# Seven block products for the recurrence's projection and the output projection

## The chip, the core and the metric

The kernel runs on one core of a Trainium2 chip. The metric is device time in microseconds for one execution of the whole kernel. The core's engines are PE (TensorE, matrix products into the eight PSUM banks), DVE (VectorE), ACT (ScalarE), POOL (GpSimd) and SP (SyncE, which issues the DMA transfers). Each engine works through its own queue in the order in which the program was written, and waits on semaphores for the others.

## The reference

One layer of an encoder block on x (1 x 1024 x 1024, float32), cut to what matters here:

```
z   = rms_norm(x) @ w_in                          # 1024 x 12288, split into the parts below
o_a = merge over 3 groups of dilated_window_attention(q, k, v)          # 1024 x 512
y_a = (o_a * silu(g_a)) @ w_proj_a                # 512 x 1024
o_b = rms_norm(o_fwd + o_bwd) * hg_norm_w * silu(g_b)                   # 1024 x 1024, gated recurrence both ways
y_b = o_b @ w_proj_b                              # 1024 x 1024
merged = sigmoid(zgate_a) * y_a + sigmoid(zgate_b) * y_b
out = x + merged @ w_out                          # 1024 x 1024
```

## The kernel before

Products of float32 accuracy are made of three products of the fast 32-bit type: an operand is split into a high part (ACT copies it into the type) and a low part (DVE or POOL subtracts the high part), and PE adds high x high, high x low and low x high into one PSUM bank. So one page of weights (128 x 512, 256 KB, loaded by SP) costs one ACT and one DVE or POOL instruction of 128x512, and each of its four 128x128 tiles is used in three matmuls of 128x512.

The program is not written by hand in its final order. A builder (`Builder`, with `Plan` as its clock) emits PE's work in sequence and, between the matmuls, those tasks of the other engines whose operands its cost model says are ready (`tick`); all times of the model only fix the order. Rings (`Ring`) are fixed numbers of buffers used in turn: `get` takes the next buffer, `done` gives it back, `soon` asks whether the next is free. All helpers record through one line, so the profile shows line 56 nearly everywhere, and instructions are told apart by tile names: `whi`, `wlo` (weights, a ring of `RING = 9` pairs), `sh`, `sl` (operands), `gp` (a PSUM bank).

The kernel has three stages. The first makes the norm and the input projection for attention, with seven block products in place of eight for many weight pages (`run_quads`). The second runs the recurrence among the remaining input projections and stores its result, per head, to a scratch in DRAM (`out_transpose`, `store(obD[h, u], t)`). The change is in the third stage, which begins where `hctx.close()` stands:

- Attention's projection: 16 units (8 column blocks j x 2 halves of the tokens) of 4 x 3 = 12 matmuls. `evac_ya` multiplies the bank by sigmoid(zgate_a) on DVE, into tile `ma`. The operand comes from scratch `oaD` (`split_load`, tiles `ld`, `sh`, `sl`), the gates from scratch `sgD` (`sig_load`, tiles `sgl`, ACT makes the sigmoid), four buffers.
- The recurrence's projection: 16 units of 8 x 3 = 24 matmuls; the operand from scratch `obD`, all 16 pages split once and kept. `evac_yb` multiplies by the gate (DVE), adds `ma` (POOL), and splits the sum for the next product (ACT `mh`, DVE `ml`). The recurrence's norm weight `hwc` is applied to the weight pages in their split (`b.scales`).
- The output projection: 16 units (8 blocks of 128 tokens x 2 halves of the columns) of 24 matmuls; `evac_out` adds x out of the bank on DVE and stores.

The order of loops is column block, then half (`for j in range(8): for half in range(2):`), so a weight page is used twice and given back. PSUM is dealt out as three banks for these units (`gps`, tile `gp`) and five for everything else (`bank`), as it was in the second stage. The weight pages of this stage are part of the kernel's one list of pages, loaded into a ring of four raw buffers in order; their low parts are made by POOL, or by DVE where there is a scale.

Of the kernel before, what the change touches and what calls it, by code (L numbers as in the profile page):

```python
# [572 lines left out]
def hybrid_block(ctx, tc, a, out):  # L573
# [69 lines left out]
    items += [wpa[i] for i in range(8)] + [wpb[i] for i in range(16)] + [wo[i] for i in range(16)]  # L643
# [5 lines left out]
    for i in range(16):  # L649
        b.scales[b.ops - 32 + i] = hwc  # L650
# [1178 lines left out]
    def out_transpose(h, u, on):  # L1829
# [5 lines left out]
        a_.activation(t, ps, AF.Copy)  # L1835
# [17 lines left out]
    OA, OB = {}, {}  # L1853
    ectx = {}

    def end_start():
        bctx.close()
        ectx["ep"] = ep = ctx.enter_context(tc.tile_pool(name="end", bufs=1))
        ectx["ld"] = b.ring(ep, "ld", 6, [128, 512])
        for k in range(8):  # L1860
            b.task("sp", [oaD], lambda k=k: split_load(OA, k % 4, k // 4, oaD[k % 4, k // 4],
                                                       lambda n: ep.tile([128, 512], F32R, tag="L", name=n, bufs=17)),
                   4, ectx["ld"].soon)

    def split_load(to, j, half, src, new):
        t = ectx["ld"].get()
        s_.dma_start(t, src)
        b.task("act", [t], lambda: split_store(to, j, half, t, new), 4)

    def split_store(to, j, half, t, new):  # L1870
        hi, lo = new(b.name("sh")), new(b.name("sl"))
        a_.activation(hi, t, AF.Copy)
        v_.tensor_tensor(lo, t, hi.bitcast(F32), op=OP.subtract)
        ectx["ld"].done(t)
        to[j, half] = (hi, lo)

    n = 0
# [11 lines left out]
    assert pos == b.ops - 40, pos  # L1889
# [4 lines left out]
    ep = ectx["ep"]  # L1894
    ob = ctx.enter_context(tc.tile_pool(name="endo", bufs=1, side="right"))
    MA, MH, ML = {}, {}, {}
    for half in range(2):
        for h in range(8):
            k = 8 * half + h
            b.task("sp", [obD], lambda h=h, half=half: split_load(  # L1900
                OB, h, half, obD[h, half], lambda n: ob.tile([128, 512], F32R, name=n)), 4, ectx["ld"].soon)
    def sig_load(w, j, half):
        t = ep.tile([128, 512], F32, tag="sg", name=b.name("sgl"), bufs=4)
        s_.dma_start(t, sgD[w, j, half])
        b.task("act", [t], lambda: (a_.activation(t, t, AF.Sigmoid), open_.add((w, j, half))), 1)
        return t

    def three(wp, xs, c):
        (wh, wl), (xh, xl) = wp, xs
        return [(wh[:, c:c + 128], xh), (wh[:, c:c + 128], xl), (wl[:, c:c + 128], xh)]  # L1910

    def evac_ya(j, half, sg):
# [29 lines left out]
    k = 0  # L1942
# [155 lines left out]
```

## Time and profile before

| | us |
|---|---|
| times of three runs | 1539.01, 1541.7, 1544.57 |
| median | 1541.7 |
| profiled execution: span from the first to the last instruction | 1541.9 |

| engine | busy us | share of the span |
|---|---|---|
| PE | 1502.3 | 97% |
| PE weight load | 1232.8 | 80% |
| DVE | 964.9 | 63% |
| ACT | 806.4 | 52% |
| POOL | 433.2 | 28% |

The span is the profiled execution's own time; nothing else of it is recorded around the instructions, and it stands 0.2 us above the median. PE's matmuls are pipelined: a row shows 0.39 us for a matmul that takes PE less from start to start. The page gives shares over the whole span; what a stage is limited by is read from windows and from the chain of waits. In a row of instructions, `out<-in` names tiles, then come shapes, the count, busy time and the mean of one, and the idle time before them with what ended it.

### The profile page before, as it was taken

What the parts mean: (1) busy time and instruction counts of PE and PEld (TensorE: products, weight loads), DVE (VectorE), ACT (ScalarE), POOL (GpSimd) and SP (SyncE); (2) the same over time, 40 slices, a digit from 0 to 9 for tenths busy, and PEclk for the clock granted to TensorE, in tenths of its full rate; (3) what the DMA queues carried; (4) which work ended last, traced back from release to release, by engine and by line L of the source; (5) the groups of instructions that cost most, each with busy time, mean ns of one, the idle gap of its engine ahead of it and who ended that gap; (6) DMA issues with size and microseconds to landing.
All of it is one profiled execution on the core that took longest, in us unless ns stands there. A gap on an engine that the chain in (4) does not pass through costs nothing. (4 is left out here: it accounts for less than half of the span.)

```text
span 1541.9 us, 22959 instructions
## 1 busy us (share of the span) xinstructions
PE 1502.3 (97%) x8109; PEld 1232.8 (80%) x8109; DVE 964.9 (63%) x1937; ACT 806.4 (52%) x1665; POOL 433.2 (28%) x424
## 2 busy tenths in 40 slices
PE   8999999999999999999989999999989999999999
PEld 7788888777778787888867788878878878888887
DVE  6791778687887834544333558889888886633211
ACT  5542667566676646776722255556554742733210
POOL 0022333232334230110113452444233432013320
PEclk9999999999999999999989999999999999999999
DMA  5443242442424457564256531131311312933232
GB/s 197 132 164 111 97 142 84 135 120 61 135 69 110 109 163 242 191 214 150 83 150 216 173 117 41 42 100 52 96 28 42 109 49 68 328 107 105 84 119 92
DMA packets 163767, 186.05 MB, mean 121 GB/s; under 512 B 42763, under 2 KB 99107, under 8 KB 163652
## 3 DMA queue, kind: packets, MB, share of 16 engines
q1 hardware_dynamic: 156228, 184.13, 38.2%
q10 hardware_dynamic: 7424, 0.45, 0.3%
q8 instruction: 64, 1.05, 0.3%
q14 instruction: 51, 0.42, 0.1%
HBM read 128.60 MB, written 60.66 MB: 123 GB/s over the span
## 5 line engine op out<-in xcount | busy, mean ns | idle before, releaser
L56 POOL TENSOR_TENSOR wlo<-raw,whi 128x512 fp32r<-128x512 f32 x119 | 160.6, 1356 | 431.6 <-ACT whi L56 412.0
L56 POOL TENSOR_TENSOR wlo<-qraw,whi 128x512 fp32r<-128x512 f32 x100 | 139.8, 1406 | 293.0 <-ACT whi L56 263.6
L56 PE MATMUL gp<-whi,hh 128*128 128x512 f32 x344 | 141.2, 411 | 2.8 <-ACT hh L56 1.4
L56 ACT ACTIVATE whi<-raw 128x512 fp32r<-128x512 f32 x136 | 85.0, 625 | 104.7 <-PE gp L56 79.4
L56 PE MATMUL gp<-hh,whi 128*128 128x512 f32 x336 | 137.8, 410 | 0.0
L56 PE MATMUL gp<-whi,hl 128*128 128x512 f32 x344 | 135.9, 395 | 1.3 <-DVE hl L56 1.3
L56 PE MATMUL gp<-wlo,hh 128*128 128x512 f32 x344 | 135.6, 394 | 0.0
L56 PE MATMUL gp<-hh,wlo 128*128 128x512 f32 x336 | 132.0, 393 | 0.0
L56 PE MATMUL gp<-hl,whi 128*128 128x512 f32 x336 | 131.6, 392 | 0.0
L56 ACT ACTIVATE whi<-qraw 128x512 fp32r<-128x512 f32 x140 | 86.0, 624 | 54.0 <-DVE qraw L56 33.6
L56 DVE CUSTOM_DVE_ANT_0 as<-sc,abias 128x192 f32<-128x192 f32 (+2 forms) x192 | 56.2, 348 | 92.8 <-PE sc L56 57.5
L56 ACT ACTIVATE stage<-gp 128x512 f32<-128x512 f32 x60 | 35.4, 594 | 113.6 <-PE gp L56 92.5
L56 ACT ACTIVATE as<-as,neg 128x192 f32<-128x192 f32 (+2 forms) x192 | 83.5, 438 | 7.9 <-DVE neg L56 7.9
L56 DVE TENSOR_TENSOR qraw<-qraw,qraw 128x512 f32<-128x512 f32 x80 | 67.3, 843 | 30.7 <-POOL wlo L56 23.6
L56 PEld LDWEIGHTS gp<-whi,hh 128*128 128x128 f32 x344 | 65.5, 190 | 24.1 <-issue 5.9
L56 PEld LDWEIGHTS gp<-whi,hl 128*128 128x128 f32 x344 | 65.4, 190 | 16.3 <-DVE hl L56 2.2
L56 PEld LDWEIGHTS gp<-wlo,hh 128*128 128x128 f32 x344 | 65.7, 191 | 12.2 <-issue 0.2
L56 PE MATMUL gp<-sh,whi 128*128 128x512 f32 x192 | 74.7, 389 | 0.0
L56 PE MATMUL gp<-sl,whi 128*128 128x512 f32 x192 | 74.7, 389 | 0.0
L56 PE MATMUL gp<-sh,wlo 128*128 128x512 f32 x192 | 74.7, 389 | 0.0
L56 PEld LDWEIGHTS gp<-hh,wlo 128*128 128x128 f32 x336 | 63.4, 189 | 14.0
L56 PEld LDWEIGHTS gp<-hh,whi 128*128 128x128 f32 x336 | 63.7, 190 | 11.4
(257 smaller groups left out, 3980.3 us busy)
## 6 DMA issues: line engine op xcount, KB each, us to landing
raw<-in_w_in_dram SPq DMA_DIRECT2D x112, 256.0 KB, 2.7
qraw<-in_w_in_dram SPq DMA_DIRECT2D x80, 256.0 KB, 4.3
qkD<-ny SPq DMA_DIRECT2D x48, 256.0 KB, 2.1
igD<-stage SPq DMA_DIRECT2D x32, 256.0 KB, 2.0
ig<-igD SPq DMA_DIRECT2D x32, 256.0 KB, 4.4
sgl<-sgD SPq DMA_DIRECT2D x32, 256.0 KB, 3.6
sgD<-stage SPq DMA_DIRECT2D x26, 256.0 KB, 2.0
ak<-qkD SPq DMA_DIRECT2D x6, 1024.0 KB, 7.9
```

Source lines behind the costliest of these rows:

```text
L56: got = f(*args, **kw)
```

## The change

Both 1024 x 1024 products of the third stage are written as 2 x 2 blocks of 512 x 512, and made from seven block products. With A the weights and X the operand, the products in their order are `SEVEN = ("11", "21", "T2", "T1", "T3", "22", "T4")`; "11", "21" and "22" use a block of the weights as it is, the T's use sums or differences of blocks, and likewise on the operand's side. Each block product is 4 x 4 tile pairs x 3 = 48 matmuls.

- Banks are held: PSUM is dealt out anew, four and four. The products 11, T2, T3, T4 add into the same four banks; 21, then T1 and 22, go into the other four. After 11, T2 and T1 ACT copies the running sum out of the bank (tiles `acc`) while it stays open; after 21, T3 and 22 DVE adds the bank to such a copy, which gives a finished quarter; T4 gives the last quarter alone.
- The sums of weights and operands (`mix`) are made by DVE in the raw tiles, one step ahead of their use, in an order of their own (`in_order`); the low parts of all pages of the stage but attention's are made by DVE (`b.low = "dve"`).
- Each operand page is split again for each product: 7 x 4 splits on the operand's side and 7 x 4 on the weights' side for each of the two products. Rings: 8 pairs `xh`/`xl` for operands, 9 pairs for weights, 18 raw weight pages (`eraw`), 8 kept sums (`acc`), 3 gate or x pages (`sg`, four before).
- In the recurrence's projection a finished quarter is multiplied by its gate (DVE, "gate") and added to `ma` by POOL ("merge"). In the output projection POOL adds x to the kept copies ("fold"), 12 instructions; for the last quarter DVE adds x out of the bank.
- Attention's loops are exchanged: half outside, column block inside.
- `hwc` is applied in the copy before the recurrence's result is stored (`out_transpose`).

The diff, cut to its core:

```diff
-    items += [wpa[i] for i in range(8)] + [wpb[i] for i in range(16)] + [wo[i] for i in range(16)]
+    items += [wpa[i] for i in range(8)]
...
-    for i in range(16):
-        b.scales[b.ops - 32 + i] = hwc
...
-        a_.activation(t, ps, AF.Copy)
+        a_.activation(t, ps, AF.Copy, scale=hwc)
...
-        ectx["ld"] = b.ring(ep, "ld", 6, [128, 512])
+        ectx["acc"] = b.ring(ep, "acc", 8, [128, 512])
+        ectx["xh"] = b.ring(ep, "xh", 8, [128, 512], F32R)
+        ectx["xl"] = b.ring(ep, "xl", 8, [128, 512], F32R)
+        ectx["sg"] = b.ring(ep, "sg", 3, [128, 512])
...
+    def split_x(t):
+        hi, lo = ectx["xh"].get(), ectx["xl"].get()
         a_.activation(hi, t, AF.Copy)
         v_.tensor_tensor(lo, t, hi.bitcast(F32), op=OP.subtract)
+        return hi, lo
...
+    psum(4)
...
+    rawq = b.ring(ob, "eraw", 18, [128, 512])
...
+    SEVEN = ("11", "21", "T2", "T1", "T3", "22", "T4")
...
+        for op in SEVEN:
+            for i in range(4):
+                m = {"T2": "11", "T1": "11", "T3": "12", "T4": "21"}.get(op, op)
+                split(op, m, i, op not in ("11", "21", "T2"))
+        for i in range(4):
+            mix("T3", i, "12", "22", "12", OP.subtract)
+            mix("T2", i, "11", "12", "11", OP.add, ("11",))
+        for i in range(4):
+            mix("T4", i, "21", "21", "11", OP.subtract, ("21",))
+            mix("T1", i, "11", "22", "11", OP.subtract, ("T2",))
+        in_order(work)
+        in_order(mixes)
...
+        for op, a, kh in (("11", 0, 0), ("21", 0, 1), ("T2", 0, 0), ("T1", 1, 0), ("T3", 0, 0), ("22", 0, 1), ("T4", 1, 1)):
+            for i in range(4):
+                split(op, kh, a, i)
+        for i in range(4):
+            mix("T3", i, (0, 0), (0, 0), (1, 0), OP.subtract, ("11",))
+            mix("T2", i, "s2", (1, 1), (0, 0), OP.subtract)
+        for i in range(4):
+            mix("T1", i, (1, 0), (1, 0), (1, 1), OP.add)
+            mix("22", i, (0, 1), (0, 1), "s2", OP.subtract, ("21",))
+        in_order(work)
+        in_order(mixes)
+        return pairs
...
+    def seven(base, pairs, tok, A, E, kept, fin, ready):
+
+        bankA, bankE, p, q, r = {}, {}, {}, {}, {}
+
+        def keep(to, op, u, ps):
+            to[u] = t = acc.get()
+            a_.activation(t, ps, AF.Copy)
+            kept(op, u, t)
+
+        def add(op, u, t, ps):
+            if ready is not None:
+                b.until(lambda: ready(op, u))
+            v_.tensor_tensor(t, ps, t, op=OP.add)
+
+        def evac(op, u):
+            if op == "11":
+                keep(p, op, u, bankA[u])
+            elif op == "21":
+                add("11", u, p[u], bankE[u])
+                E.done(bankE[u])
+                fin(0, 0, u, p[u], None)
+            elif op == "T2":
+                keep(q, op, u, bankA[u])
+            elif op == "T1":
+                keep(r, op, u, bankE[u])
+            elif op == "T3":
+                add("T1", u, r[u], bankA[u])
+                fin(1, 1, u, r[u], None)
+            elif op == "22":
+                add("T2", u, q[u], bankE[u])
+                E.done(bankE[u])
+                fin(0, 1, u, q[u], None)
+            else:
+                fin(1, 0, u, bankA[u], A)
+
+        for o, op in enumerate(SEVEN):
+            for u in range(4):
+                if op == "11":
+                    bankA[u] = A.get(name="sA")
+                elif op in ("21", "T1"):
+                    bankE[u] = E.get(name="sE")
+                out = (bankE if op in ("21", "T1", "22") else bankA)[u]
+                for k in range(4):
+                    n = base + 4 * o + (k if tok else u)
+                    b.until(lambda: b.split_next > n and (op, k) in pairs)
+                    (wh, wl), (xh, xl) = b.w[n], pairs[op, k]
+                    if tok:
+                        s = slice(128 * u, 128 * u + 128)
+                        prods = [(xh[:, s], wh), (xh[:, s], wl), (xl[:, s], wh)]
+                    else:
+                        s = slice(128 * k, 128 * k + 128)
+                        prods = [(wh[:, s], xh), (wh[:, s], xl), (wl[:, s], xh)]
+                    for i, (l, x) in enumerate(prods):
+                        t_.matmul(out, l, x, start=(op in ("11", "21", "T1") and k == 0 and i == 0),
+                                  stop=(k == 3 and i == 2), skip_group_check=op in ("T2", "T3", "22", "T4"))
+                    if tok and u == 3:
+                        b.free_to(n + 1)
+                    if u == 3:
+                        drop_x(pairs[op, k])
+                    b.tick()
+                if not tok:
+                    b.free_to(n + 1)
+                evac(op, u)
+                b.tick()
...
+    b.low = "dve"
+    seven_weights(b.ops, wB, (obs[:8], obs[8:], ()))
+    pairs_b = seven_sides(X)
...
+    seven_weights(b.ops + 28, wO)
+
+    def fin_b(half, c, u, t, bank_):
+        j = 4 * c + u
+        sg = (1, j, half)
+
+        def gate():
+            d = t if bank_ is None else sgs[sg]
+            v_.tensor_tensor(d, t, sgs[sg], op=OP.mult)
+            if bank_ is None:
+                sgr.done(sgs[sg])
+            else:
+                bank_.done(t)
+            b.task("pool", [d], lambda: merge(d), 2)
+
+        def merge(d):
+            ma = MA[j, half]
+            g_.tensor_tensor(ma, d, ma, op=OP.add)
+            (acc if bank_ is None else sgr).done(d)
+            M[half, c, u] = ma
+
+        b.task("dve", [t], gate, 1, lambda: sg in open_)
+
+    seven(b.ops, pairs_b, False, b.gps, b.bank, lambda *_: None, fin_b, None)
...
+    def fold(op, u, t):
+        def f():
+            g_.tensor_tensor(t, t, xr[op, u], op=OP.add)
+            sgr.done(xr[op, u])
+            folded.add((op, u))
+        b.task("pool", [t], f, 1, lambda: (op, u) in xr and b.when_all([xr[op, u]]))
...
+    def fin_o(half, e, u, t, bank_):
+        r0 = 128 * (4 * half + u)
+        ring, o = acc, t
+        if bank_ is not None:
+            b.until(lambda: ("T4", u) in xr)
+            ring, o = sgr, xr["T4", u]
+            v_.tensor_tensor(o, t, o, op=OP.add)
+            bank_.done(t)
+
+        def out_():
+            s_.dma_start(out[r0:r0 + 128, 512 * e:512 * e + 512], o)
+            ring.done(o)
+        b.task("sp", [o], out_, 1)
+
+    seven(b.ops + 28, pairs_o, True, b.bank, b.gps, fold, fin_o, lambda op, u: (op, u) in folded)
```

More of the change, by code (lines that the diff above doesn't have):

```diff
@@ L1888, in hybrid_block @@
     hctx.close()
-    assert pos == b.ops - 40, pos
-    ep = ectx["ep"]
+    assert pos == b.ops - 8, pos
+    psum(4)
+    ep, acc, sgr = ectx["ep"], ectx["acc"], ectx["sg"]
     ob = ctx.enter_context(tc.tile_pool(name="endo", bufs=1, side="right"))
[L1896 to L1901, printed above, removed]
+    rawq = b.ring(ob, "eraw", 18, [128, 512])
@@ L1963, in evac_out @@
[L1963 to L1993 removed]
+    AT = (("21", 0, 0), ("T3", 1, 1), ("22", 0, 1), ("T4", 1, 0))
```

202 lines of the change are left out of this document (117 added, 85 removed).

## The prediction

> **What bounds the kernel now.** I read the page first: the span, the busy shares, the 40 slices.
>
> ```profile
> span 1541.9 us, 22959 instructions
> PE 1502.3 (97%) x8109; PEld 1232.8 (80%) x8109; DVE 964.9 (63%) x1937; ACT 806.4 (52%) x1665; POOL 433.2 (28%) x424
> ...
> PE   8999999999999999999989999999989999999999
> ...
> DVE  6791778687887834544333558889888886633211
> ...
> PEclk9999999999999999999989999999999999999999
> ```
>
> PE is busy in nine tenths of every late slice at full clock; VectorE (DVE) falls to 2, 1, 1 tenths in the last three. Next the chain that ended last, its last steps:
>
> ```profile
> 1308.45 229.88 PE gp L56 x1014
> ...
> 1538.36 0.69 DVE stage L56
> ```
>
> For the last 230 us nothing but PE's own queue is on the path. The change touches the end of that stretch; the table by windows splits it into attention projection, recurrence projection (call it B) and output projection (O):
>
> ```profile
> core 0: us, PE busy (x) PEld busy (x) DVE busy (x) ACT busy (x) POOL busy (x), PEclk, DMA share, GB/s
> 1320.30:1364.00 43.70, 43.70 (x194) 36.18 (x193) 27.38 (x42) 27.16 (x45) 0.10 (x1) 1.00 0.77 255
> 1364.00:1451.00 87.00, 87.00 (x386) 72.03 (x385) 27.24 (x39) 26.88 (x46) 29.59 (x23) 1.00 0.30 94
> 1451.00:1541.90 90.90, 87.32 (x386) 71.97 (x384) 12.44 (x18) 5.58 (x9) 11.64 (x9) 1.00 0.35 107
> ```
>
> In all three PE is busy throughout. VectorE has 27, 27 and 12 us of work beside 44, 87 and 91: lots of room, and this room is what the change spends. The matmuls of the three parts, in the view of one tile (each has three kinds of equal count; the first and the last are shown):
>
> ```profile
> L56 PE MATMUL gp<-sh,whi x192: 389/389/389, 1320.6 to 1450.4; 128*128 128x512 f32 x192
> ...
> L56 PE MATMUL gp<-whi,ml x128: 388/389/389, 1451.6 to 1537.9; 128*128 128x512 f32 x128
> ```
>
> 3 x 192 + 3 x 128 = 960 matmuls start between 1320.6 and 1537.9: 217.3 / 959 = 0.2266 us each. That pace prices everything that PE loses or gains.
>
> **Part by part: what goes.** Attention's 192 matmuls stay. B and O have 384 each; seven block products of 4 x 4 tile pairs x 3 are 336 each. 96 matmuls go: 96 x 0.2266 = 21.8 us, if PE stays fed. One block product lasts 48 x 0.2266 = 10.88 us. The scale of the recurrence's norm moves into an existing copy; that costs nothing that PE could wait for.
>
> **What comes: VectorE.** Each operand page, on both sides and for each of the seven products, is split into a high part (ScalarE) and a low part (VectorE), and there are sums before the splits and after the products. Rows for the price of one:
>
> ```profile
> 1333.96 1.29 DVE L56 TENSOR_TENSOR sl<-ld,sh 128x512 fp32r<-128x512 f32 x2
> 1335.17 1.28 DVE L56 TENSOR_TENSOR ma<-gp,sgl 128x512 f32<-128x512 f32 x2
> ...
> L56 DVE TENSOR_TENSOR stage<-gp,xr 128x512 f32<-128x512 f32 x16 | 11.1, 692 | 73.2 <-PE gp L56 73.2
> ```
>
> A lone 128x512 addition is shown as 0.69 us, but two end within 1.29, and the pair at 1333.96 gives way to the next at 1335.17: 1.21 / 2 = 0.605 us per addition when they queue.
>
> In the order in which the changed program's instructions stand, VectorE's queue from the first low part of B's second product ("21") to the low part of the last weight page that O's fourth product ("T1") needs holds 177 instructions of 128x512: 81 low parts, 64 sums of operands and weights, 16 additions out of PSUM banks, 16 gate multiplications (four of these out of PSUM). The first cannot start before attention's last matmul: its buffer is one of a ring of eight pairs, still held by attention's operand. The last is wanted by PE ten products and ten matmuls after that moment: 10 x 10.88 + 2.3 = 111.1 us. VectorE needs 177 x 0.605 = 107.1 us, so even with nothing else it would be within 4 us of being the bound. ScalarE has some 12 instructions per product, and rows for it are
>
> ```profile
> 1340.15 0.63 ACT L56 ACTIVATE sh<-ld 128x512 fp32r<-128x512 f32 x1 [0.53 <-DMA ld<-obD]
> 1340.82 0.69 DVE L56 TENSOR_TENSOR sl<-ld,sh 128x512 fp32r<-128x512 f32 x1 [0.16 <-ACT sh L56]
> ...
> 1348.88 1.66 ACT L56 ACTIVATE sgl<-sgl 128x512 f32<-128x512 f32 x3
> ```
>
> Three in 1.66 us, 0.55 each: 6.6 of 10.88 us, not the bound. The first two rows show the handover: a high part at 1340.15, its low part 0.67 later. The held banks cost nothing: the two sets of four take turns, so each copy or addition out of a bank has a whole product, 10.88 us, before PE writes there again.
>
> **GpSimd's share of VectorE's time.** The program keeps 16 merges on GpSimd and adds 12 of its additions (the residual into kept partial products); 24 of the 28 lie within those 177. Rows:
>
> ```profile
> L56 POOL TENSOR_TENSOR sgl<-sgl,ma x16: 1283/1284/1289, 1370.6 to 1452.2; 128x512 f32<-128x512 f32 x16
> ...
> 1156.18 1.28 POOL L56 TENSOR_TENSOR km<-km,sk 128x512 f32<-128x512 f32 x1
> 1156.28 1.20 DVE L56 SCALAR_TENSOR_TENSOR rr<-rt,ri 128x4 f32<-128x4 f32 x1
> ...
> 1157.91 0.16 DVE L56 SCALAR_TENSOR_TENSOR rr<-rt,rr 128x4 f32<-128x4 f32 x1
> ...
> 1319.12 1.29 POOL L56 TENSOR_TENSOR wlo<-raw,whi 128x512 fp32r<-128x512 f32 x1 [6.71 <-DMA ld<-oaD]
> ...
> 1319.54 1.42 DVE L56 TENSOR_TENSOR sl<-ld,sh 128x512 fp32r<-128x512 f32 x1 [0.34 <-ACT sh L56]
> ...
> L56 DVE TENSOR_TENSOR spare<-qC,spare x12: 677/688/692, 159.7 to 496.1; 128x512 f32<-128x512 f32 x12
> ```
>
> GpSimd takes 1.28 us for one. A VectorE instruction of 128x4 that takes 0.16 us took 1.20 when it came 0.10 behind one: 1.04 us lost, until GpSimd was done. A low part that came 0.42 behind took 1.42 instead of 0.69. An addition out of a PSUM bank was never over 692 ns in the twelve of one group. So behind a queue that never empties each GpSimd addition takes about 1.04 us from VectorE: 24 x 1.04 = 25.0 us. Bounds: 0.5 each (12 us) if half of them fall on PSUM additions or on VectorE's own waits; 1.28 each (30.7 us) if all are met at their start.
>
> The Trainium skill, "SBUF — State Buffer", section "SBUF: two separate sides", says that a VectorE operation with two SBUF inputs and a GpSimd operation that reads SBUF take turns for the whole instruction, and the loser blocks fully. The rows agree in kind (1.20 instead of 0.16; nothing for PSUM sources). By its letter the sum has 30.7 for 25.0, 5.7 us more.
>
> **VectorE's own waits.** In four places of the 177 a low part stands directly behind the sum it is made of, and ScalarE must make the high part in between: about 0.75 us each; in six one instruction stands between: 0.15 each. That is 3.9. At the start the weight pages of "21" are loaded behind gate pages that wait for one of three buffers, and landing takes
>
> ```profile
> DMA to landing us min/median/max: 2.9/3.6/5.4
> ```
>
> one landing, of which I count 3 us (SP's queue is in order: the operand pages stand behind that gate page too). Together 7, bounds 2 and 12. ScalarE's first high part takes 0.7. Sum: 0.7 + 107.1 + 25.0 + 7 = 139.8 us, against 111.1: PE is 28.7 us late by O's "T1". Behind that stand 32 VectorE instructions for four products, 4.8 us in each 10.88, and PE runs freely again; lateness is not regained.
>
> A nearer point shows how this begins. The addition that empties the last bank of B's "21" can run 0.4 us after that product, at 22.2 us. From it to the low part that B's "T1" begins with are 28 instructions: 28 x 0.605 = 16.9, two GpSimd merges 2.1, two of the 0.75 waits and two of 0.15 1.8, and 0.1 until it lands: 43.1, where PE wants it at 32.6. So 10 us of the 28.7 are lost by there, about 3 inside "T2" and 7 in one gap before "T1".
>
> **The border.** The PSUM banks are dealt out anew before attention's projection, and its first matmul now waits for ScalarE's copy out of the last bank before it.
>
> ```profile
> 1320.33 0.39 PE L56 MATMUL gp<-hh,wlo 128*128 128x512 f32 x1
> ...
> 1320.56 0.39 PE L56 MATMUL gp<-sh,whi 128*128 128x512 f32 x1
> ...
> 1320.81 0.60 ACT L56 ACTIVATE stage<-gp 128x512 f32<-128x512 f32 x1 [1.30 <-issue]
> ```
>
> The copy ends at 1321.41; the matmul stood at 1320.56 and can then start at about 1321.5: 1.0 us once (bounds 0.8 and 1.3), with all of attention's matmuls queued behind it. At the far end nothing changes: a VectorE addition out of PSUM and one store behind the last matmul.
>
> **PE's clock after a gap.** Three windows around the one long gap of the trace:
>
> ```profile
> 1238.40:1241.50 3.10, 0.22 (x2) 0.02 (x1) 3.03 (x7) 0.43 (x1) 1.28 (x1) 1.00 0.10 18
> 1241.60:1244.90 3.30, 3.02 (x14) 3.02 (x15) 0.23 (x1) 0.00 (x0) 0.00 (x0) 0.50 0.15 57
> 1245.00:1248.30 3.30, 3.30 (x26) 3.04 (x25) 1.60 (x7) 0.60 (x1) 0.00 (x0) 1.00 0.00 0
> ```
>
> PE was busy 0.22 of the first 3.1 us; the next 3.3 us ran at 0.50, with 14 matmuls for 26 in the third. Half of 3.3 is lost: 1.7 us. Most of it is hidden where PE waits for VectorE again anyway; the last stall, in O's "T1", has no such cover, and may come in pieces of 1 to 4 us. I take 0.9, bounds 0 and 3.4.
>
> **The sum.** The profiled execution has a span of 1541.9 us; the median of three runs is 1541.7 (1539.01 to 1544.57), so the span stands for the median. -21.8 + 28.7 + 1.0 + 0.9 = +8.8: **1550.7 us**.
>
> **The rivals.** *PE stays nearly fed, and the kernel is faster.* If GpSimd's additions cost VectorE nothing (they fall into its waits, or on additions out of PSUM), only the sequence at B's "T1" remains: 22.2 + 16.9 + 1.8 + 0.1 = 41.0 against 32.6, 8.4 us, plus 2.0 at O's start (its first low part stands behind a weight page that needs the buffer of B's last one: 0.67 + 0.605 + 0.7), plus the border and 0.9. -21.8 + 8.4 + 2.0 + 1.0 + 0.9 = -9.5: 1532.4. For it: VectorE is 31% busy in B's window now, and the additions out of PSUM do run freely. Against it: the 1.20 and 1.42 rows, and a queue that is within 4 us of full without GpSimd. It decides at about 0.67 us for each of the 24: 24 x 0.67 = 16.1 is 8.9 less than 25.0, all of the forecast's loss. Chance 0.14.
>
> *The clock bites.* Four gaps (before B's "T1", O's start, O's "T2" and "T1") that each outlast 3 us and are followed by matmuls that PE cannot make up: 4 x 1.7 = 6.8 instead of 0.9: 1556.6. For it: the 0.50 row. Against it: while PE is behind VectorE's queue a slow matmul costs nothing. Chance 0.16.
> The Trainium skill, "TensorE: Matmul & The Clock Gate", Part 1, has the clock halved after an idle window of about 3.4 us until a busy one has passed; the 3.1 us window with its 0.22 us of work and the 0.50 row behind it agree.
>
> *The sums are not in time for lack of data.* In attention's window DMA moves 255 GB/s at a share of 0.77; the changed program also loads there the operand of B, and behind it two more sets of weight pages. If B's third product waits some 10 us longer for pages, VectorE's whole queue shifts: 1560.7. Against it: the same 255 GB/s already holds a similar number of pages. Chance 0.10.
>
> **How the numbers follow.** My forecast has 0.60. A measurement tells 0.3%, 4.6 us, from no change; "same" is 1537 to 1546. Forecast bounds: GpSimd 12 to 30.7 moves it by -13 to +5.7, waits by -5 to +5, clock by -0.9 to +2.5; not all at once, so 1540 to 1559 for it alone. The range 1540 to 1562 leaves out the faster rival (0.14) and the far end of the data rival. Faster: the first rival nearly whole and a sliver of the forecast, 0.14; same: the forecast's low end, 0.16; slower: 0.70.
>
> **What would show it.** In the changed profile: about 864 matmuls from the border to the end; VectorE over 90% busy from B's second product to O's fourth; GpSimd rows of 1.28 beside VectorE additions of 1.3 to 1.9 us; a PE gap of about 7 us before B's "T1", released by the low part of a weight page, and several of 1 to 5 us at O's start, "T2" and "T1"; clock 0.5 behind the long one; a first attention matmul about 1 us behind its predecessor. I am wrong if PE stays above 95% busy there, if VectorE additions stay at 0.69 beside GpSimd's, or if PE's waits name DMA or ScalarE's copies out of the held banks.

## The result, and the profile after

The changed kernel takes 1553.98 us (median of four runs, 1549.17 to 1556.16) against 1541.28 us for the kernel before beside it: a ratio of 1.0078, 95% interval 1.0055 to 1.0101, so 12.7 us slower. 1550.7 was forecast, in a range of 1540 to 1562. The page of the profiled execution (its own time is 1549.17 us):

```profile
span 1546.9 us, 22973 instructions
PE 1486.8 (96%) x8013; PEld 1216.6 (79%) x8013; DVE 1065.4 (69%) x2077; ACT 845.6 (55%) x1737; POOL 437.2 (28%) x420
...
DVE  6791777787877835454333459889798885378984
```

96 matmuls are gone (8013 for 8109) and PE is busy 15.5 us less, but the kernel is longer. VectorE's last three slices, once 2, 1, 1 tenths, are 9, 8 and 4. The span is only 5.0 us longer than before's, less than the medians say: attention's first matmul starts 5.7 us earlier, behind stages that the change hardly touches. PE's clock fits that: ahead of this matmul it stood at 0.50 for 20.5 us in the profiled execution of before, and for 3.4 in this one. The same place in the table by windows (columns as in the next table), of before (first row) and of after:

```profile
797.80:808.00 10.20, 9.81 (x20) 5.91 (x21) 6.77 (x8) 1.98 (x3) 2.00 (x2) 0.50 0.18 69
```
```profile
798.30:801.70 3.40, 3.40 (x8) 1.93 (x8) 1.84 (x3) 0.00 (x0) 1.27 (x1) 0.50 0.00 0
```

So I compare the changed stretch itself, from the start of attention's first matmul to the start of the last matmul ("the stage" below): 217.4 us before (1320.56 to 1537.93), 228.1 after (1314.84 to 1542.97). With the border in front of it, where the time between the starts of two matmuls grew from 0.23 to 1.23 us, that is 11.7 us, near the 12.7 of the medians. In the table by windows of after, the rows are attention's end, B's "11" and "21", B's "T2" with the gap before "T1", the rest of B, O's first four products, and O's last three:

```profile
core 0: us, PE busy (x) PEld busy (x) DVE busy (x) ACT busy (x) POOL busy (x), PEclk, DMA share, GB/s
1336.60:1358.40 21.80, 21.80 (x98) 18.07 (x97) 10.66 (x17) 10.06 (x17) 0.00 (x0) 1.00 0.60 193
1358.40:1380.20 21.80, 21.80 (x98) 18.07 (x97) 17.87 (x29) 9.60 (x17) 1.75 (x2) 1.00 0.78 273
1380.20:1403.90 23.70, 14.12 (x49) 10.33 (x48) 19.86 (x31) 11.14 (x20) 4.47 (x3) 0.83 0.13 34
1403.90:1451.80 47.90, 46.34 (x192) 37.76 (x192) 43.78 (x62) 25.53 (x46) 14.68 (x10) 0.94 0.40 126
1451.80:1510.50 58.70, 49.47 (x192) 39.23 (x193) 51.30 (x66) 25.46 (x48) 22.71 (x14) 0.88 0.24 77
1510.50:1543.20 32.70, 32.70 (x145) 26.89 (x144) 15.96 (x26) 6.74 (x13) 2.37 (x1) 1.00 0.32 113
```

Where the row's length and PE's busy time differ, PE stands: in B's "T2" and before "T1", in O's first four products, and for 1.6 us in the rest of B. PEclk below 1.00 marks the same rows. Seven products at 10.88 us, twice, behind attention's 43.6 would end the stage at 195.7; 32.4 us are lost, at six places: B's "T2" with the gap behind it 12.8 and "T1" 2.6, the passage to O 1.8, O's "11" 6.0, "T2" 0.8, "T1" 8.4. PE's new waits in the view of waits (total, times, longest):

```profile
PE sE L56 <- ACT whi L56: 9.9, 2, 6.0
...
PE sA L56 <- DVE xl L56: 4.0, 2, 3.7
PE sA L56 <- ACT whi L56: 3.6, 1, 3.6
...
PE sA L56 <- ACT xh L56: 1.6, 1, 1.6
...
PE sE L56 <- DVE wlo L56: 1.2, 1, 1.2
```

They name high and low parts, as the forecast wanted, not the copies out of the held banks. And the border, in the timeline:

```profile
1314.10 0.60 ACT L56 ACTIVATE stage<-gp 128x512 f32<-128x512 f32 x1 [0.81 <-PE gp L56]
...
1314.84 0.47 PE L56 MATMUL gp<-xh,whi 128*128 128x512 f32 x1 [0.84 <-ACT stage L56]
```

### The profile page after: what moved, and what is told of

Read it like the earlier page. It is cut to its first block, busy times and chain, and to the rows that moved or that the text cites. A ratio compares the mean times of both kernels' runs of the same rounds, so it can differ in the third digit from the quotient of the medians.

```text
span 1546.9 us, 22973 instructions
## 1 busy us (share of the span) xinstructions
PE 1486.8 (96%) x8013; PEld 1216.6 (79%) x8013; DVE 1065.4 (69%) x2077; ACT 845.6 (55%) x1737; POOL 437.2 (28%) x420
## 5 line engine op out<-in xcount | busy, mean ns | idle before, releaser
L56 POOL TENSOR_TENSOR wlo<-raw,whi 128x512 fp32r<-128x512 f32 x103 | 139.9, 1365 | 383.4 <-ACT whi L56 372.2
L56 ACT ACTIVATE whi<-raw 128x512 fp32r<-128x512 f32 x120 | 74.9, 626 | 68.9 <-PE gp L56 42.9
L56 PEld LDWEIGHTS gp<-hh,whi 128*128 128x128 f32 x336 | 63.5, 189 | 11.2
L56 PEld LDWEIGHTS gp<-hl,whi 128*128 128x128 f32 x336 | 63.4, 189 | 11.0
L56 POOL COPY mm<-Bc 128x4 f32<-128x4 f32 x96 | 41.2, 468 | 83.2 <-DVE Bc L56 81.7
L56 ACT ACTIVATE ny<-spare 128x512 f32<-128x512 f32 x50 | 31.3, 626 | 58.8 <-DVE spare L56 58.8
```

What stands on the lines that cost most here:

```text
L56: got = f(*args, **kw)
```

## The experiments

Three causes were to be told apart: GpSimd's additions that hold VectorE up (A, the prediction's); VectorE's order of work (D, its nearer point at B's "T1"); and, once the first four runs were in, late operand pages of B (E). The clock was tested last. In the recorded expectations of e1 to e4 three rivals have letters of their own: Rival B is the order and the rings without GpSimd, Rival C is ScalarE's queue behind a late gate page, and the Rival D of e3 is only that VectorE has too much work. The table has, for each run, the stage and the start of six products in us after attention's first matmul, read from the profiled execution's matmuls; the first row is PE without a gap.

| run | stage | B "T1" | B "T3" | O "11" | O "21" | O "T1" | O "T3" | time, median | ratio to before, 95% |
|---|---|---|---|---|---|---|---|---|---|
| (no gap) | 195.7 | 76.3 | 87.2 | 119.8 | 130.7 | 152.4 | 163.3 | | |
| after | 228.1 | 89.1 | 102.6 | 137.0 | 153.9 | 176.5 | 195.7 | 1553.98 | 1.0078 (1.0055 to 1.0101) |
| e1_small_pool | 212.8 | 88.5 | 102.2 | 136.0 | 147.4 | 169.2 | 180.4 | 1536.05 | 0.9976 (0.9960 to 0.9992) |
| e2_adds_on_dve | 219.1 | 87.7 | 100.1 | 134.0 | 146.9 | 169.5 | 186.7 | 1543.87 | 1.0024 (1.0008 to 1.0040) |
| e3_low_on_pool | 239.4 | 89.2 | 103.1 | 136.9 | 151.6 | 185.5 | 207.0 | 1565.91 | 1.0173 (1.0153 to 1.0193) |
| e4_four_gates | 225.9 | 89.0 | 102.3 | 136.9 | 156.2 | 178.0 | 193.5 | 1550.88 | 1.0075 (1.0048 to 1.0102) |
| e5_operand_first | 215.4 | 76.3 | 88.2 | 126.0 | 144.1 | 165.8 | 183.0 | 1541.28 | 1.0000 (0.9988 to 1.0013) |
| e6_all_three | 202.7 | 76.3 | 87.2 | 121.0 | 137.6 | 159.4 | 170.3 | 1528.86 | 0.9912 (0.9895 to 0.9928) |
| e7_order_only | 217.9 | 86.4 | 97.3 | 133.6 | 152.8 | 174.6 | 185.5 | 1543.12 | one run |
| e8_keep_warm | 230.8 | 94.5 | 105.5 | 139.4 | 157.6 | 179.4 | 198.3 | 1556.89 | 1.0094 (1.0079 to 1.0109) |
| e9_keep_warm_short | 223.2 | 88.8 | 100.0 | 134.4 | 149.9 | 175.5 | 190.8 | 1545.96 | 1.0031 (1.0017 to 1.0046) |
| e10_operand_and_order | 208.8 | 76.3 | 87.2 | 125.6 | 143.7 | 165.5 | 176.4 | 1534.25 | 0.9957 (0.9940 to 0.9973) |
| e11_operand_and_adds | 212.1 | 76.3 | 87.2 | 122.4 | 139.7 | 161.5 | 179.7 | 1535.87 | 0.9976 (0.9959 to 0.9994) |

The kernel before took 1539.8, 1541.7 and 1539.8 us in the three groups of runs (e1 to e4, e5 to e8, e9 to e11); each ratio is to its own group. The changed kernel was timed beside its own runs of before alone.

### GpSimd's additions: e1, e2, e3

e1 cuts the 28 additions to 4 of their 512 columns, leaves the rest of those sums out, and leaves each instruction in its place:

```
-            g_.tensor_tensor(ma, d, ma, op=OP.add)
+            g_.real.tensor_tensor(ma[:, 0:4], d[:, 0:4], ma[:, 0:4], op=OP.add)
...
-            g_.tensor_tensor(t, t, xr[op, u], op=OP.add)
+            g_.real.tensor_tensor(t[:, 0:4], t[:, 0:4], xr[op, u][:, 0:4], op=OP.add)
```

> GpSimd's 28 additions of the last stage (16 merges, 12 folds) are cut to 4 of their 512 columns; the rest of those sums is left out. Every instruction of every engine keeps its place. Stage = first matmul of attention's projection to the last matmul: 217.4 us before, 228.1 in the changed kernel. Theory A (GpSimd's additions hold VectorE up, about 1.04 us each for the 24 that lie in its long queue): 25 us of VectorE's time go; PE still waits some 10 us at the recurrence's T1, so the stage is 208 to 213 us and the kernel some 16 us faster than the changed one, about 1537. Rival B (the waits come from the order, the rings and ScalarE's queue; GpSimd only coincides): stage within 4 us of 228.

e2 gives the same 28 additions, whole, to VectorE:

```
-            b.task("pool", [d], lambda: merge(d), 2)
+            b.task("dve", [d], lambda: merge(d), 2)
...
-            g_.tensor_tensor(ma, d, ma, op=OP.add)
+            v_.tensor_tensor(ma, d, ma, op=OP.add)
...
-            g_.tensor_tensor(t, t, xr[op, u], op=OP.add)
+            v_.tensor_tensor(t, t, xr[op, u], op=OP.add)
...
-        b.task("pool", [t], f, 1, lambda: (op, u) in xr and b.when_all([xr[op, u]]))
+        b.task("dve", [t], f, 1, lambda: (op, u) in xr and b.when_all([xr[op, u]]))
```

> The same 28 additions, whole, are made by VectorE instead of GpSimd. Theory A: each costs VectorE 0.605 us instead of about 1.04, so the 24 in the long queue cost 14.5 instead of 25: stage about 218 us, kernel about 1544. Rival B: VectorE's queue is longer by 17 us of work and nothing is taken off it: stage 232 or more, kernel 1558 or more.

e3 goes the other way and makes the low parts of the weights on GpSimd:

```
-    b.low = "dve"
+    b.low = "pool"
```

> The low parts of the 56 weight pages of the two products are made by GpSimd instead of VectorE. Theory A: each takes 1.04 us or more from VectorE by holding it up, in place of 0.605: 37 of them lie in the long queue, +16 us: stage about 244 us, kernel about 1570. Rival D (VectorE simply has too much work, and GpSimd is free capacity): 37 x 0.605 = 22 us go from VectorE's queue: stage 206 to 212, kernel about 1534.

Stages of 212.8, 219.1 and 239.4 us: 15.3 and 9.0 less than the changed kernel, and 11.3 more, where 16 was expected. Groups of instructions on VectorE and GpSimd from 1358 us on (busy, mean ns of one), after:

```profile
L56 DVE TENSOR_TENSOR wlo<-eraw,whi 128x512 fp32r<-128x512 f32 x51 | 39.9, 802 | 15.5 <-ACT whi L56 15.2
L56 DVE TENSOR_TENSOR eraw<-eraw,eraw 128x512 f32<-128x512 f32 x32 | 27.2, 855 | 0.0
L56 DVE TENSOR_TENSOR xl<-ma,xh 128x512 fp32r<-128x512 f32 x24 | 19.6, 850 | 0.2 <-ACT xh L56 0.2
...
L56 DVE TENSOR_TENSOR acc<-sE,acc 128x512 f32<-128x512 f32 x12 | 8.1, 679 | 0.0
...
L56 POOL TENSOR_TENSOR ma<-acc,ma 128x512 f32<-128x512 f32 x12 | 18.5, 1547 | 116.5 <-DVE acc L56 116.5
```

and in e1:

```profile
L56 DVE TENSOR_TENSOR wlo<-eraw,whi 128x512 fp32r<-128x512 f32 x50 | 33.3, 687 | 15.7 <-ACT whi L56 15.4
L56 DVE TENSOR_TENSOR eraw<-eraw,eraw 128x512 f32<-128x512 f32 x32 | 21.7, 682 | 0.0
L56 DVE TENSOR_TENSOR xl<-ma,xh 128x512 fp32r<-128x512 f32 x24 | 15.6, 683 | 0.4 <-ACT xh L56 0.4
```

With whole additions on GpSimd, VectorE's three largest groups between SBUF tiles take 802 to 855 ns in the mean; with small ones 682 to 687. The group that reads a PSUM bank takes 679, and 682 in e1. GpSimd pays too: 1.55 us in the mean of this group, where one alone took 1.28. One turn in the timeline of after, in which VectorE's instruction takes 1.77 us and ends 0.5 behind GpSimd's:

```profile
1461.53 1.72 POOL L56 TENSOR_TENSOR acc<-acc,sg 128x512 f32<-128x512 f32 x1 [1.18 <-issue]
...
1462.02 1.77 DVE L56 TENSOR_TENSOR eraw<-eraw,eraw 128x512 f32<-128x512 f32 x1
```

VectorE waited only 0.8 us, once, for a result of GpSimd, so it is the turns and not late results. So A holds, and e2 says what it is worth to a program that computes everything: the stage is 9.0 us shorter with 28 more additions on VectorE (28 x 0.605 = 16.9 us). The price of the turns alone doesn't give that much: the 24 additions in the long queue would take 14.5 us on VectorE, and their turns took at most 19.6 (worked out below). VectorE also waits less for high parts in e2 (7.0 us instead of 15.2 from 1358 to 1525 us), and PE's clock stands at 0.50 for 13.7 us of the stage instead of 27.3; how much each is worth stays open. The table shows where e1 gains: nearly all of it lies in O ("11" 11.4 us long instead of 16.9, "T1" 11.2 instead of 19.2). B is nearly untouched: "T1" starts at 88.5 instead of 89.1. The loss in B, nearly half of all, is not GpSimd's.

### What holds B up: e4, e5, e7

The chain of waits of after, at that place:

```profile
1358.86 0.61 DVE ma L56
...
1359.53 0.32 SPq L56
...
1362.26 5.11 DMA ob<-obD
...
1367.47 0.70 DVE acc L56
...
1382.83 2.63 DMA sg<-sgD
...
1386.19 0.53 ACT whi L56
...
1386.77 1.22 PE sA L56 x2
```

and SyncE's queue in the timeline of after:

```profile
1357.09 0.42 SPq L56 DMA_DIRECT2D eraw<-in_w_proj_b_dram  x1
1359.53 0.32 SPq L56 DMA_DIRECT2D sg<-sgD  x1
1359.90 0.42 SPq L56 DMA_DIRECT2D eraw<-in_w_proj_b_dram  x1
1360.37 3.87 SPq L56 DMA_DIRECT2D ob<-obD  x8
```

SyncE issues in the order of its program. A gate page (sg) needs one of three buffers. The page issued at 1359.53 waited for one that VectorE frees with the last gate multiplication of attention's projection (DVE ma, 1358.86 in the chain); the second half of B's operand (ob, eight pages) stands behind it and is issued from 1360.37 on, though its last data were written to memory by an issue at 1302.5. The page on the chain is there at 1367.37, 8.9 us after B's first matmul (1358.48). VectorE is idle 1.7 us until then, and then works for 13 us nearly without a pause; 12 of its first 20 instructions are operand sums and their low parts, which it could have made earlier.

e4 gives the gate pages a fourth buffer (and takes one of eighteen from the weight pages):

```
-        ectx["sg"] = b.ring(ep, "sg", 3, [128, 512])
+        ectx["sg"] = b.ring(ep, "sg", 4, [128, 512])
...
-    rawq = b.ring(ob, "eraw", 18, [128, 512])
+    rawq = b.ring(ob, "eraw", 17, [128, 512])
```

> Four buffers for gate pages and x pages instead of three, and 17 raw weight buffers instead of 18 (there is no room for both). Theory A: VectorE sets the pace, no change: stage 225 to 231. Rival C (ScalarE stands in its queue on a sigmoid whose gate page had to wait for one of three buffers, with the weights' high parts behind it; the chain of the changed kernel shows this ahead of the 4.0 us gap in the recurrence's T2): that gap and its like go, 4 to 8 us: stage 220 to 224.

It did next to nothing: "T1" at 89.0, ratio 1.0075 for the changed kernel's 1.0078, and a stage (225.9) inside what was expected for no change. The operand pages' row in its trace (first and last issue) shows why:

```profile
L56 SPq DMA_DIRECT2D ob<-obD x16: 423/428/443, 1336.8 to 1368.3; - x16
```

The last operand page is issued 49.3 us after attention's first matmul (1318.99); in after it was 48.9 (1363.7). The queue is as before, with one more gate page ahead, and the operand still behind it. Nor did Rival C get what it needs: ScalarE still waits 3.6 us for a gate page, up to 1387.22, with the high part that opens B's "T2" (1387.76) behind it. This run speaks for neither side, since its edit did not move what it was to move.

e5 puts the operand's pages ahead of the gate pages, and of B's weight pages too, by one number in one line:

```
-                b.task("sp", [obD], f, 2, b.wire)
+                b.task("sp", [obD], f, 0.5, b.wire)
```

> The changed kernel with one edit: the pages of B's operand (its second half) go into SyncE's queue ahead of the gate pages that wait for one of three buffers, instead of behind them. Everything is computed. Where the four runs before leave it: B's loss (T2 10.9 to 12.8 us, T1 2.6) stood untouched by GpSimd's additions, so it is not theirs. Theory E (B's operand arrives too late: its last pages are issued in order behind gate pages, and VectorE has nothing to do at B's start): B's T1 begins at about 76 us after attention's first matmul instead of 89.1, O begins at 125 to 127 instead of 137.0; O's own loss remains and may even grow by 1 to 3 us, since VectorE's queue is as long as before, so the stage is 215 to 219 us instead of 228.1 and the time 1540 to 1545 us (ratio to before 1.000 to 1.003). Theory D, the prediction's own step (B's T1 is late by VectorE's order of 28 instructions and two holds by GpSimd): T1 still begins 10 us late, at 86 to 89 us, stage 225 to 228, time 1549 to 1553 us.

The pages' rows in after, and in e5:

```profile
L56 SPq DMA_DIRECT2D ob<-obD x16: 422/428/1077, 1329.9 to 1363.7; - x16
L56 DVE TENSOR_TENSOR ob<-ob,ob x8: 683/684/1189, 1365.1 to 1397.7; 128x512 f32<-128x512 f32 x8
```
```profile
L56 SPq DMA_DIRECT2D ob<-obD x16: 383/430/442, 1320.3 to 1343.2; - x16
L56 DVE TENSOR_TENSOR ob<-ob,ob x8: 681/684/690, 1347.6 to 1376.7; 128x512 f32<-128x512 f32 x8
```

Counted from attention's first matmul (1314.84 and 1320.00), the last page is issued at 23.2 instead of 48.9 us and the first sum begins at 27.6 instead of 50.3. B's "T1" starts at 76.3, without a gap, with the same number of instructions on VectorE; the stage is 12.7 us shorter. E holds. Landing takes no less than in after (3.9 us in the median, 3.7 there), so the pages were late for their place in the queue and not for the load on DMA. D, that order and holds alone would keep "T1" 10 us late, falls. And the three gate buffers are still three, so the gate page that ScalarE stands behind in after (the chain at 1382.83) looks late because VectorE, late itself, freed its buffer late.

e7 changes VectorE's order alone: operand sums for "22", and the splits of "T3" and "22", wait until the weights of "T1" are split, and the sums for "22" come behind all of those for "T1".

```
-                         and b.when_all([at()]) and ectx["xh"].soon() and ectx["xl"].soon(), f))
+                         and b.when_all([at()]) and (op not in ("T3", "22") or b.split_next >= base + 16) and ectx["xh"].soon() and ectx["xl"].soon(), f))
...
-                           and near([X[*k, i] for k in at]) and (op != "T2" or acc.soon()), f))
+                           and near([X[*k, i] for k in at]) and (op != "T2" or acc.soon()) and (op != "22" or b.split_next >= base + 16), f))
...
             mix("T1", i, (1, 0), (1, 0), (1, 1), OP.add)
+        for i in range(4):
             mix("22", i, (0, 1), (0, 1), "s2", OP.subtract, ("21",))
```

> The changed kernel with the order edit alone: operand sums for '22', and the splits of 'T3' and '22' operands, behind the splits of T1's weight pages; everything is computed. Theory E with a queue at O (order is a small part): B's T1 3 to 4 us earlier than 89.1, O's T1 product 13 us long instead of 19.2, stage 221 to 223 us instead of 228.1, time 1543 to 1548 us. Theory D (order is the cause of B's late T1): B's T1 at 79 to 81 us, stage about 218 us, time 1539 to 1543 us. If VectorE's queue is late as a whole and order is indifferent: stage 226 to 229 us, time 1549 to 1553 us.

217.9, in a single run: a larger gain than E expected (221 to 223), and D's figure for the stage, but not D's for B: "T1" comes 2.7 us earlier, not 8 to 10, and the whole wait moves into "T2" (one gap of 8.1 us). Most of what e7 gains it gains at "T1", where nothing is lost any more in either projection: 2.6 and 8.4 us in after. At O's start it loses 4.3 us more. So order is not what makes VectorE late in B; it decides whether work that nobody waits for yet stands ahead of work that PE waits for. I had undersized that.

### PE's clock: e8, e9

Dummy matmuls of 128x128 keep PE busy where it stood, written into banks that PE is about to open, so that the next matmul overwrites them (e8: 30, 52, 32 and 36 at the four places; e9: 17, 25, 15 and 18).

```
+        def keep_warm(where, n):
+            if where not in early:
+                early[where] = E.get(name="sE")
+            for _ in range(n):
+                t_.real.matmul(early[where][:, 0:128], ident, ident, start=True, stop=True)
...
+                if first and (op, u) == ("T2", 1):
+                    keep_warm(("T1", 0), 30)
+                if first and (op, u) == ("T1", 0):
+                    early[op, u] = bankE[u]
+                    keep_warm((op, u), 52)
+                    early.pop((op, u))
...
+                    if not first and (op, u, k) == ("T1", 0, 3):
+                        keep_warm((op, 1), 36)
...
+                        if not first and (op, u, k, i) == ("11", 0, 0, 2):
+                            keep_warm(("21", 0), 32)
```

> The changed kernel with dummy matmuls of 128x128 where TensorE has its gaps: 30 before T2's second unit and 52 before T1's first in B, 32 in O's 11 and 36 in O's T1, all into PSUM banks that TensorE is about to open, so that their result is overwritten; the other engines do the same work in the same order, and everything is computed. The gaps stay as late as they were, but TensorE is not idle in them. Theory 'clock' (each gap is followed by 6.8 us at clock 0.5, and at least the last, in O's T1, is not made up): no window at 0.5 at the four places, and the stage 2.7 to 6 us shorter than 228.1, 222 to 225.5 us, time 1547 to 1550 us, ratio to before 1.004 to 1.006. Theory 'the slow clock is hidden where TensorE waits for VectorE again anyway' (the prediction's 0.9 us): stage 227 to 228, time 1550 to 1553 us, ratio 1.007 to 1.009. If the dummy matmuls outlast the gaps, T1 in B begins later than 89.1 and the stage is longer than 228.1.

e8 did not decide: each dummy left two records of some 0.11 us, and 6.6 to 11.5 us of them outlasted gaps of 4.0 to 6.3 us. B's "T1" was pushed to 94.5, the stage to 230.8; what full clock gave and what the dummies took can't be parted there.

> As e8_keep_warm, with half as many dummy matmuls: there each 128x128 matmul of fp32 ran as two records of about 0.11 us, so 30, 52, 32 and 36 of them took 6.6, 11.5, 7.0 and 7.9 us, longer than the gaps that they were to fill, and delayed T1 in B to 94.5 us instead of 89.1. Now 17, 25, 15 and 18: estimated at 3.8, 5.5, 3.3 and 4.0 us, a little less than the gaps of 4.0, 6.3, 4.1 and 4.3 us. Everything is computed. Theory 'clock' (the 6.8 us at clock 0.5 behind the last gap are not made up): clock 1.0 at all four places, O's T1 product some 16 us long instead of 19.2, stage 223 to 226 us instead of 228.1, ratio to before 1.003 to 1.006. Theory 'VectorE's queue alone sets the ends' (a slow clock is hidden where TensorE waits again): O's T1 product still 18.5 to 19.2 us, stage 227 to 229 us, ratio 1.006 to 1.009.

O's last gap in after, in the table by windows (columns as above), and the same place in e9:

```profile
1494.60:1498.00 3.40, 0.50 (x1) 0.19 (x1) 3.40 (x5) 1.24 (x3) 0.97 (x1) 1.00 0.51 152
1498.00:1504.80 6.80, 5.62 (x13) 4.47 (x14) 4.14 (x7) 2.58 (x5) 2.16 (x1) 0.50 0.06 18
```
```profile
1494.00:1498.00 4.00, 4.00 (x37) 3.96 (x36) 4.00 (x6) 3.38 (x7) 1.65 (x1) 1.00 0.39 117
1498.00:1504.80 6.80, 6.74 (x31) 5.39 (x30) 3.54 (x6) 1.49 (x3) 3.95 (x2) 1.00 0.14 42
```

13 matmuls in 6.8 us at half clock against 31 (in the first, 1.2 us of the time is a wait for a low part). All four stretches at 0.50 are gone (a new one of 3.4 us came in O's "T2"), and the stage is 223.2: full clock at the four places was worth 4.9 us, net of what the dummies took, and the ratio to before is 1.0031 (1.0017 to 1.0046), clear of the changed kernel's interval. O's "T1" product took 15.3 us, where the theory of the clock had 16 and the other 18.5 to 19.2. The other theory is right about the stretches before it: e9 leads by 4.0 us at O's "21" and by 1.0 at "T1" (the table), because "T2" took 14.7 us instead of 11.7: PE, earlier, waited for VectorE there, and ran 3.4 us of it at 0.50.

### Together: e10, e11, e6

e10 has the edits of e5 and e7, e11 those of e5 and e2, e6 all three.

> The changed kernel with the operand pages of B ahead of the gate pages and with the order edit, GpSimd's 28 additions left where they are; everything is computed. Alone the two took 12.7 and 10.2 us from the stage of 228.1; all three edits left 202.7. If the two losses are separate, 22.9 us go: stage about 205 us. If order mostly moved the same lateness (what it took at B was the operand's), only its part at O is left, 4 to 7 us: stage 208 to 212 us, time 1533 to 1537 us, ratio 0.994 to 0.997. And GpSimd's additions then still cost the difference to 202.7, 5 to 9 us, about all of it at O's start, where VectorE's queue stays full.

> The changed kernel with the operand pages of B ahead of the gate pages and GpSimd's 28 additions on VectorE, without the order edit; everything is computed. Alone the two took 12.7 and 9.0 us. If they are separate, as theory E and the holds say (operand at B, holds at O): stage 206 to 210 us, B's T1 at 76.3, O's T1 product still 15 to 18 us long for want of the order edit, time 1530 to 1535 us, ratio 0.993 to 0.996. If VectorE's queue only shifts its lateness from one product to the next: stage 213 us or more, ratio 0.998 or more.

> The changed kernel with three edits, everything computed: the operand pages of B ahead of the gate pages (as in the run before this one), the 28 additions of GpSimd on VectorE (as in e2_adds_on_dve), and VectorE's sums and splits reordered so that those of '22' and the splits of 'T3' and '22' stand behind the splits of T1's weight pages. If the three losses are separate and each edit takes its own away (operand late 13 us, GpSimd's holds 9 net of the moved work, order 4 or so): stage 202 to 205 us instead of 228.1, 24 us less, the time 1526 to 1530 us, ratio to before 0.991 to 0.993. If VectorE's queue as a whole is the bound, and the edits only shift which product waits (the loss removed at B comes back at O): stage 212 to 219 us, time 1536 to 1543 us, ratio 0.998 to 1.002.

Alone the three edits take 12.7 (operand), 10.2 (order) and 9.0 us (additions) from the stage; in pairs 19.3 and 16.0 instead of 22.9 and 21.7; together 25.4 instead of 31.9. So they are mostly separate, and a part looks like one lateness that each of them can take away. e10 came out as the second of its expectations, and its 6.1 us behind e6 stand at O's "21" already (143.7 and 137.6): GpSimd's additions at O's start; e11 (212.1) lies between its two, nearer the one in which VectorE's queue shifts its lateness on. e6 is 0.9912 of before (0.9895 to 0.9928), 12.8 us faster than the kernel before and 25 faster than the changed one. Its chain through B:

```profile
1366.15 10.88 PE sA L56 x48
1377.03 10.88 PE sE L56 x48
1387.91 10.88 PE sA L56 x48
1398.79 10.88 PE sE L56 x48
```

"11", "21", "T2" and "T1" are back to back. What is left of the loss is 7 us at O's start, where VectorE is full; 2.7 of them are the clock's, since the 46 matmuls behind the last wait took 13.1 us, where 10.4 would do. The table by windows of e6:

```profile
1443.30:1492.70 49.40, 46.42 (x193) 37.90 (x194) 47.89 (x80) 24.06 (x44) 0.00 (x0) 0.93 0.26 84
```

80 instructions, 47.9 of 49.4 us: VectorE's queue, which the prediction priced, now makes PE wait there alone.

## Why the prediction was right, and where it was not

**The matmuls, the border: as forecast.** 864 matmuls start in the stage, 96 fewer; a product without a gap takes 10.88 us in every run. The border cost 1.00 us for a forecast of 1.0.

**VectorE's queue: right in its length, wrong in what it is made of.** The forecast had the low part that O's "T1" needs 139.8 us behind attention's end, where PE wants it at 111.1. In after that matmul, the fourth page's second, starts at 1499.18, 140.7 us behind B's first at 1358.48. One row holds the stretch:

```profile
1358.40:1498.90 140.50, 120.41 (x492) 96.23 (x490) 128.46 (x180) 67.08 (x121) 38.86 (x24) 0.92 0.37 119
```

180 VectorE instructions for 177 counted, 24 GpSimd additions for 24, VectorE 91% busy. But the terms: 180 x 0.605 is 108.9, so GpSimd's turns made at most 19.6 us of the 128.5 (0.82 each, not 1.04: 25.0), and VectorE stood 12.0 us, not 7. The two errors, each about 5 us, nearly cancel: that the total came out is in part luck.
The Trainium skill, "SBUF — State Buffer", section "SBUF: two separate sides", with turns of a whole instruction, gives 30.7 for that term (an estimate, 24 x 1.28). The trace agrees with it in kind (802 to 855 ns against 679 for PSUM sources, and GpSimd's own 1.55 for 1.28) and not in amount. In the timeline of that stretch 21 VectorE instructions last longer than 0.69 us, by 18.2 us in all (near the 19.6), and each ends 0.55 us behind an addition of GpSimd. Ten of the 24 additions have an instruction that reads PSUM beside them and cost VectorE 0.39 us in the mean, three of these nothing; the other 14 cost 1.02, nearly the forecast's 1.04. So the price of a full turn was right; that every addition would take a full turn was not.

**The step that failed: the nearer point.** It had B's "T1" 10 us late from 28 instructions and two of GpSimd's merges, and took 3 us for the landing of one page at the start. The lateness was there (12.8 us), the cause was not: e1 removes the merges and "T1" stays; e5 moves the pages and it vanishes. I saw in the order of instructions that the operand pages stand behind the gate page and priced that as one landing. It was eight pages behind a page that waits for a buffer that attention's own end frees, and the sums behind them could have been done in VectorE's free time (10.66 of 21.8 us busy in the last stretch of attention). The rival on late data (0.10) came nearest: it named late pages, though from the load on DMA and not from the order of the queue, and put the 10 us on top of the forecast's; it should have stood in place of that step.

The same error stands in the queue's start, which the prediction set at attention's last matmul. In e5 the low part for O's "T1" comes 129.0 us behind B's first matmul, instead of 140.7, with GpSimd's turns left as they were:

```profile
1363.60:1492.50 128.90, 115.44 (x491) 92.56 (x490) 121.42 (x170) 62.94 (x117) 38.77 (x23) 0.96 0.34 110
```

170 VectorE instructions stand in that stretch for 180, and it is idle 7.5 us for 12.0. In the last 21.8 us of attention e5 has 27 VectorE instructions for 17. So the 177 instructions did not all have to stand behind attention's end.

**The clock: undersized.** 0.9 us was taken, bounds 0 and 3.4; e9 shows 4.9. Behind O's last gap nothing hides it: the 38 matmuls from 1499.18 to the end of that product (1510.56) took 11.4 us instead of 8.6, 2.8 lost. The rest comes from the earlier stretches: in e9 the matmul that waits for the low part starts 182.0 us into the stage instead of 184.3. That slow matmuls empty the banks later, and so feed VectorE's queue later, would explain this; it was not tested by itself. The rival "the clock bites" with 6.8 us was nearer.

**The sum.** -21.8 + 29.6 (PE's lateness at that matmul: 140.7 less 111.1) + 2.8 + 1.0 = +11.6, against +8.8: of the 2.8 missed, 1.9 is the clock behind the last gap and 0.9 the queue, in which the clock of the earlier stretches is contained. The medians differ by 12.7.

Of what was to be seen, the gap before B's "T1" (6.3 us, 7 forecast) was released by a high part instead of a low part, and O's "T2" had hardly a gap; the gaps at O's start and "T1" came as said.

## What to carry to other kernels

When work moves to an engine that has room on average, list what that work waits for, down to the DMA queue that brings it: a page that nobody waited for becomes the head of the new queue, and in an in-order queue it stands behind every page that waits for a buffer. A queue's total can be right for wrong reasons; a forecast of where the first gap opens, and an experiment that moves one cause at a time, tell which. Here the fewer matmuls gained nothing with the loads fitted alone (1.0000), 0.4% and 0.2% with order or engine fitted too (e10, e11), and 0.9% with all three (e6).

## What was not expected of the hardware

PE's clock does not need a long gap to halve. In e9's O "T2", where matmuls came 1.3, 0.8 and 0.5 us apart at three places and 0.2 to 0.3 otherwise, in the table by windows:

```profile
1479.30:1482.70 3.40, 2.09 (x7) 1.16 (x7) 3.40 (x7) 2.44 (x5) 0.00 (x0) 1.00 0.38 142
1482.70:1486.10 3.40, 3.40 (x9) 2.62 (x8) 3.40 (x6) 0.40 (x2) 1.68 (x1) 0.50 0.32 104
```

PE was busy 2.09 of 3.4 us and the next 3.4 ran at 0.50, 9 matmuls for some 15. A window of 2.14 us busy was not followed by half clock (e5, 1485.8 to 1489.2), so the border, if there is a sharp one, lies near these two figures. And each of the four gaps of after, of 4.0 to 6.3 us, was followed by 6.8 us at 0.50, two such stretches. The Trainium skill, "TensorE: Matmul & The Clock Gate", Part 1, has the clock halved after at least one idle window of about 3.4 us; here a window that was 61% busy was enough. So small stalls in a row can be dearer than their sum: that "T2" took 3.8 us more than 10.88, of which the stalls are 2.1 and the half clock 1.7.
